# Windowed attention: values and probabilities as two rounded parts each, low keys on all 128 rows, normalisation on POOL

## The chip, the cores and the metric

One core of a Trainium2 chip. The metric is the device time of one execution in microseconds (us). The core has the engines PE (matrix products), DVE and ACT (elementwise work and copies out of PSUM, where PE leaves its results), POOL (elementwise work) and SP (here it only issues transfers). Each works through its own list of instructions in the order in which the program emits them, and semaphores between the engines hold an instruction until its inputs are there and its output's place is free.

## The reference

Two layers over 640 tokens (512 sample tokens, 128 prompt tokens) of width 1024. A layer is a SwiGLU half step, a mixer, and another half step, each followed by a LayerNorm. The mixer of layer 0 is the attention that is changed; that of layer 1 is a long convolution.

```python
def attn_latent(h, k_ctx, v_ctx, w_qkv, w_o, sink):
    q, k, v = split_qkv(h, w_qkv)          # 16 query heads, 4 key heads, 64 wide
    q, k = rope_2d(q), rope_2d(k)
...
    def block(b):                          # 128 queries
        ...
        valid = (jnp.abs(qi[:, None] - kj[None, :]) <= WINDOW) & (kj >= 0)[None] & (kj < L)[None]
        s_loc = jnp.einsum('bqkgd,bskd->bkgqs', qb, kb).astype(jnp.float32) * ATTN_SCALE
        s_loc = jnp.where(valid, s_loc, NEG_INF)
        s_ctx = jnp.einsum('bqkgd,bckd->bkgqc', qb, k_ctx).astype(jnp.float32) * ATTN_SCALE
        p = jax.nn.softmax(jnp.concatenate([s_loc, s_ctx, sink_logits(sink, B, BLOCK)], -1), axis=-1)
        o = (jnp.einsum('bkgqs,bskd->bqkgd', p[..., :S].astype(vb.dtype), vb)
             + jnp.einsum('bkgqc,bckd->bqkgd', p[..., S:S + Lc].astype(v_ctx.dtype), v_ctx))
    return o @ w_o
```

The prompt's 128 tokens attend to themselves in the same way, with no rotation and no window.

## The kernel before, in words

The program is emitted in one order for all engines, written out by hand, and each engine runs its share of it in that order. No scheduler moves anything; only pieces of LayerNorm and of the rotation (`rope`) are placed by an emission clock (`clk`, `at`, `run_due`), which counts the time of PE's products.

Products are made from float32 values in two parts that are each rounded to the type float32r: `split` copies the value into a float32r tile (the high part, on ACT) and subtracts (the low part, on DVE or POOL). A product is then three matmuls: high by high, high by low, low by high.

`attn` works in this order. `qstep` and `kstep` make the queries and keys in halves of 320 tokens; `rope` copies them from PSUM (`qs`), rotates them, and `q_hi`, `q_lo`, `k_hi`, `k_lo` write the parts. `q_lo` has two DVE operations for a half, of 320 columns for the first and of 192 for the second. Then 20 groups follow, each of four heads `g` of one block `b` of 128 queries: blocks 1 and 2 see 512 keys, blocks 0 and 3 see 384, and the prompt (block 4) sees 128. The main loop has 22 iterations of four slots. Slot i of iteration n holds, in this order:

- `tr` for chunk i of group n-2: four transposes of the probabilities `p` into the PSUM tile `pt` on PE, and a copy of it to `pts` on ACT. A group has as many chunks as its width holds 128s.
- `score` for head i of group n: two matmuls on PE (`kh` with the query, `kl` with its high half) into `s`, then on DVE one operation that adds the mask and takes the row's extreme (`tensor_tensor_reduce`, in the trace a custom operation, "p<-s,mask,sinkn"), then on ACT the exponential, which needs that extreme (`sm`).
- in the first two iterations, five steps of the values' product (`vstep`).
- `norm` of the heads of group n-1 (DVE), spread over the slots as 1, 2, 1, 0.
- `av` for an earlier chunk: one float32 matmul of `pts` with 64 columns of values, into one half of the PSUM tile `o`; the two groups of a pair (g even, g odd) fill its halves. After a pair's last chunk ACT copies `o` to `osb`, POOL makes the parts `oh` and `ol` of three heads, ACT and POOL those of the fourth.

So 58 slots hold both a chunk and a score: 28 with a score of 512 columns, 18 with 384, 12 with 128. Iterations 0 and 1 have scores without chunks, as do the slots behind a group's last chunk: after the first chunk there are 4 such scores of 512 columns, 6 of 384 and 4 of 128. After iteration N-3 the output projection's first weights are split on POOL (`w_split(nc.gpsimd, nc.gpsimd)`).

Of the kernel before, what the change touches and what calls it, by code (L numbers as in the profile page):

```python
# [15 lines left out]
P = 128  # L16
T = 640
# [25 lines left out]
class Kernel:  # L43
# [133 lines left out]
    def ada_first(self):  # L177
        """shift and scale of the first sub-layer: rows on the tensor engine, then columns"""
# [54 lines left out]
    def bg_step(self):  # L233
        """128 columns of one mod: dot products along the free dimension"""
# [22 lines left out]
    def sh(self, l, i):  # L257
        """columns for the modulated input of the sub-layer that follows LayerNorm i of layer l (i = -1: the input)"""
# [25 lines left out]
    def h_stages(self, half, k, src, G, B, first=False):  # L284
        """modulate, then split, as stages that the caller interleaves over k"""
# [26 lines left out]
    def interleave(self, chains, key=None, dt=0.0):  # L312
        """stage s of chain k in step k + s"""
# [74 lines left out]
    def ln_out(self, l, i, half, sum_t):  # L388
        """the last LayerNorm, to the output"""
# [80 lines left out]
    def rstd(self, vp, C):  # L470
        """1 / sqrt(variance + eps) of C x 4 tokens, on the diagonals of four C x C blocks"""
# [31 lines left out]
    def mm_cols(self, ps, w, c0, rhs, ks, half, first=True, last=True):  # L503
        """ps = w[:, ks, c0:c0+128]^T rhs[ks] over one half of the tokens"""
# [11 lines left out]
    def run_steps(self, steps, bg=False):  # L516
        """steps: (unit, fn(weights), last use)"""
# [101 lines left out]
    def rope(self, ps, half, hi, lo, raw_prompt):  # L619
        """rotate the sample tokens of one half, then hi(x, columns) and lo(x, columns); the prompt's stay as they are"""  # L620
# [15 lines left out]
        def add():  # L636
            nc.vector.tensor_tensor(out=qs[:, 0:n], in0=qs[:, 0:n], in1=st.pop("sh")[:, 0:n], op=ALU.add)
            hi(qs[:, 0:n], slice(a, s1))

        def low():  # L640
            lo(qs[:, 0:n], slice(a, s1))
# [5 lines left out]
    def attn(self, u0):  # L647
# [4 lines left out]
        v = fp.tile([P, 6, 256], F32, name="v")  # L652
        kp = fp.tile([P, 2, P], F32, name="kp")
        qp = fp.tile([P, KD, P], F32, name="qp")
        self.rcos = fp.tile([P, LS], F32, name="rcos")
        self.rsin = fp.tile([P, LS], F32, name="rsin")
        kc = self.t((P, 2, P), name="kc")
        nc.sync.dma_start(out=self.rcos, in_=I["k_cos"])
        nc.sync.dma_start(out=self.rsin, in_=I["k_sin"])
        nc.sync.dma_start(out=kc, in_=I["kcT"])  # L660
        nc.sync.dma_start(out=v[:, 0, :], in_=I["vc"])
# [5 lines left out]
        R = [slice(0, 64), slice(64, P)]  # L667

# [13 lines left out]
        def k_lo(x, c, t):  # L682
            for r in range(2):
                nc.vector.tensor_tensor(out=kl[R[r], t, c], in0=x[R[r]], in1=kh[t][R[r], r, c].bitcast(F32), op=ALU.subtract)

        def qstep(w, uu, half):
            self.flush(f"ln{half}")
            for j2 in range(2):
                jt = min(uu - u0, 3) * 2 + j2
                if jt not in q:  # L690
                    q[jt] = (self.b((P, LS), F32R, name="q0"), self.b((P, LS), F32R, name="q1"))
                ps = self.ps(name="q")
                self.mm_cols(ps, w, j2 * P, self.h, [(k, k) for k in range(KD)], half)
                self.rope(ps, half, lambda x, c, jt=jt: q_hi(x, c, q[jt]), lambda x, c, jt=jt: q_lo(x, c, q[jt]), qp[:, jt, :])

        def kstep(w, uu, half):
            for t in range(2):
                ps = self.ps(name="k")
                self.mm_cols(ps, w, t * P, self.h, [(k, k) for k in range(KD)], half)
                def col(c):  # L700
                    return slice(P + c.start, P + c.stop)

                self.rope(ps, half, lambda x, c, t=t: k_hi(x, col(c), t), lambda x, c, t=t: k_lo(x, col(c), t), kp[:, t, :])
# [5 lines left out]
        kl = self.rp.tile([P, 2, 768], F32R, tag="wr", name="kl")  # L709
        self.wlim = u + 6  # L710
        self.w_dma(u + 6)
        kh = [self.wp.tile([P, 2, 768], F32R, tag="w", name="kh") for _ in range(2)]
        for o in (0, 640):
            for t in range(2):
                k_hi(kc[:, t], slice(o, o + P), t)
                k_lo(kc[:, t], slice(o, o + P), t)
        self.wmax = 2
# [9 lines left out]
        def vstep(tt):  # L727
# [6 lines left out]
            nc.scalar.activation(out=v[:, 1 + tt, :], in_=ps[:, 0:256], func=AF.Copy)  # L734
            if tt == 4:
                nc.sync.dma_start(out=O["nv"], in_=v[:, 5, :])
# [5 lines left out]
        # block b of queries: first key column, width, first mask block, blocks of v  # L742
        WIN = [(0, 384, 6, [0, 1, 2]), (0, 512, 0, [0, 1, 2, 3]), (256, 512, 1, [2, 3, 4, 0]), (384, 384, 5, [3, 4, 0]), None]
# [7 lines left out]
        pts = {}  # L751

        def score(b, g, i):
            t, r = g // 2, g % 2
            jt = 4 * t + i
            rr = slice(64 * r, 64 * r + 64)
# [6 lines left out]
            if b < 4:  # L763
                c0, n, mb, _ = WIN[b]
                x = q[jt][r][:, b * P:b * P + P]
                nc.tensor.matmul(ps[:, 0:n], x, kh[t][:, r, c0:c0 + n], start=True, stop=False)
                nc.tensor.matmul(ps[:, 0:n], x[rr], kl[rr, t, c0:c0 + n], start=False, stop=True)
            else:
                n, mb = P, 0
                nc.tensor.matmul(ps[:, 0:n], qp[rr, jt, :], kp[rr, t, :])  # L770
# [9 lines left out]
        def norm(b, g, i):  # L780
# [4 lines left out]
            p = live[b, g][:, i, 0:WIN[b][1] if b < 4 else P]  # L785
            nc.vector.tensor_scalar(out=p, in0=p, scalar1=s[:, 3, i:i + 1], scalar2=None, op0=ALU.mult)
# [3 lines left out]
        def tr(b, g, c):  # L790
# [3 lines left out]
            x = self.t(name="pts")  # L794
            nc.scalar.activation(out=x, in_=pt, func=AF.Copy)
            pts[b, g, c] = x

        def av(b, g, c):
            t, r = g // 2, g % 2
            vs = WIN[b][3] if b < 4 else [5]  # L800
            if r == 0 and c == 0:
                ops[b, t] = self.ps(name="o")
            ob = ops[b, t]
            nc.tensor.matmul(ob[64 * r:64 * r + 64, :], v[:, vs[c], g * 64:(g + 1) * 64], pts.pop((b, g, c)),
                             start=(c == 0), stop=(c == len(vs) - 1))
            if c == len(vs) - 1:
                live.pop((b, g))
            if r == 1 and c == len(vs) - 1:
                ops.pop((b, t))
                osb = self.t(name="osb")  # L810
# [953 lines left out]
```

## Time and profile before

| what | value |
|---|---|
| three runs | 2789.57, 2790.73, 2800.66 us; median 2790.73 |
| the profiled execution: span | 2795.8 us |
| busy in the span: PE, DVE, ACT, POOL | 97%, 60%, 31%, 21% |
| attention's main part, 768 to 904 us: busy PE, DVE, ACT, POOL | 135.42, 83.44, 90.64, 27.31 us of 136 |

The span runs from the first instruction to the last. The page does not say which run was profiled; its span lies 5.1 us above the median of the runs, so differences are worked out against the span and then set on the median. Times in the trace count from the span's start.

### The profile page before, as it was taken

What the parts mean: (1) busy time and instruction counts of PE and PEld (TensorE: products, weight loads), DVE (VectorE), ACT (ScalarE), POOL (GpSimd) and SP (SyncE); (2) the same over time, 40 slices, a digit from 0 to 9 for tenths busy, and PEclk for the clock granted to TensorE, in tenths of its full rate; (3) what the DMA queues carried; (4) which work ended last, traced back from release to release, by engine and by line L of the source; (5) the groups of instructions that cost most, each with busy time, mean ns of one, the idle gap of its engine ahead of it and who ended that gap; (6) DMA issues with size and microseconds to landing.
All of it is one profiled execution on the core that took longest, in us unless ns stands there. A gap on an engine that the chain in (4) does not pass through costs nothing. (4 is left out here: it accounts for less than half of the span.)

```text
span 2795.8 us, 42366 instructions
## 1 busy us (share of the span) xinstructions
PE 2711.5 (97%) x17402; PEld 2529.1 (90%) x17402; DVE 1683.4 (60%) x3041; ACT 878.8 (31%) x1507; POOL 579.0 (21%) x639
## 2 busy tenths in 40 slices
PE   9989999998999999999999999999999899999997
PEld 3569999998844999999999999998998899999997
DVE  5865867748865567676766633337658856323334
ACT  3552222214565341212133121224332333122222
POOL 3541000005212420000041000005108842000002
PEclk8889999999999999999999999999999999999998
DMA  6343544421000235353522312121223321212121
GB/s 239 107 157 106 196 151 158 166 83 66 35 1 31 76 117 177 136 181 136 177 72 97 130 61 87 65 91 47 91 87 123 130 81 65 87 61 91 61 76 38
DMA packets 65017, 289.35 MB, mean 103 GB/s; under 512 B 8255, under 2 KB 13583, under 8 KB 46520
## 3 DMA queue, kind: packets, MB, share of 16 engines
q1 hardware_dynamic: 45736, 217.39, 22.2%
q0 software_dynamic: 18720, 69.21, 7.0%
q8 instruction: 137, 2.24, 0.3%
q14 instruction: 56, 0.46, 0.0%
q10 hardware_dynamic: 368, 0.04, 0.0%
HBM read 270.61 MB, written 16.01 MB: 103 GB/s over the span
## 5 line engine op out<-in xcount | busy, mean ns | idle before, releaser
L512 PE MATMUL f<-al,wh 128*128 128x320 f32 (+2 forms) x1408 | 437.2, 310 | 2.1 <-DVE al L94 1.6
L512 PE MATMUL f<-ah,wh 128*128 128x320 f32 (+2 forms) x1408 | 437.9, 311 | 0.0
L553 PE MATMUL g<-hh,wh 128*128 128x320 f32 (+1 forms) x1408 | 437.2, 310 | 0.0
L512 PE MATMUL f<-ah,wl 128*128 128x320 f32 (+2 forms) x1408 | 436.4, 310 | 0.0
L553 PE MATMUL g<-hl,wh 128*128 128x320 f32 (+1 forms) x1408 | 435.5, 309 | 0.0
L553 PE MATMUL g<-hh,wl 128*128 128x320 f32 (+1 forms) x1408 | 435.2, 309 | 0.0
L553 PE MATMUL u<-hl,wh 128*128 128x320 f32 (+1 forms) x1408 | 435.1, 309 | 0.0
L553 PE MATMUL u<-hh,wl 128*128 128x320 f32 (+1 forms) x1408 | 435.1, 309 | 0.0
L553 PE MATMUL u<-hh,wh 128*128 128x320 f32 (+1 forms) x1408 | 435.0, 309 | 0.0
L93 ACT ACTIVATE wh<-wr 128x2048 fp32r<-128x2048 f32 (+1 forms) x167 | 297.5, 1783 | 437.4 <-PE f L512 341.2
L94 DVE TENSOR_TENSOR wl<-wr,wh 128x2048 fp32r<-128x2048 f32 (+1 forms) x156 | 333.5, 2138 | 90.6 <-ACT wh L93 90.1
L563 DVE TENSOR_TENSOR ac<-sg,u 128x320 f32<-128x320 f32 (+1 forms) x176 | 85.8, 487 | 457.6 <-ACT sg L561 457.3
L561 ACT ACTIVATE sg<-g 128x320 f32<-128x320 f32 (+1 forms) x176 | 76.7, 436 | 768.1 <-PE g L553 768.1
L493 DVE SCALAR_TENSOR_TENSOR x<-f,gate,x 128x128 f32<-128x128 f32 (+3 forms) x432 | 172.1, 435 | 204.5 <-PE f L512 204.5
L512 PEld LDWEIGHTS f<-al,wh 128*128 128x128 f32 x1408 | 265.5, 189 | 3.9 <-DVE al L94 3.8
L512 PEld LDWEIGHTS f<-ah,wh 128*128 128x128 f32 x1408 | 265.7, 189 | 1.0 <-ACT ah L93 0.5
L512 PEld LDWEIGHTS f<-ah,wl 128*128 128x128 f32 x1408 | 265.6, 189 | 0.0
L553 PEld LDWEIGHTS g<-hl,wh 128*128 128x128 f32 x1408 | 264.5, 188 | 1.2 <-POOL hl L308 0.5
L553 PEld LDWEIGHTS g<-hh,wh 128*128 128x128 f32 x1408 | 264.4, 188 | 0.8 <-issue 0.3
L553 PEld LDWEIGHTS g<-hh,wl 128*128 128x128 f32 x1408 | 264.4, 188 | 0.1
L553 PEld LDWEIGHTS u<-hh,wh 128*128 128x128 f32 x1408 | 264.4, 188 | 0.0
L553 PEld LDWEIGHTS u<-hh,wl 128*128 128x128 f32 x1408 | 264.3, 188 | 0.0
(303 smaller groups left out, 4816.5 us busy)
## 6 DMA issues: line engine op xcount, KB each, us to landing
wr<-w SPq DMA_DIRECT2D x88, 1024.0 KB
ar<-ada_w POOLq DMA_DIRECT2D x128, 512.0 KB, 3.8
wr<-w2a SPq DMA_DIRECT2D x48, 768.0 KB
wr<-hyin SPq DMA_DIRECT2D x12, 1024.0 KB
wr<-ada_first SPq DMA_DIRECT2D x8, 1024.0 KB
specs<-sg SPq DMA_DIRECT2D x16, 512.0 KB
wr<-w2b SPq DMA_DIRECT2D x8, 1024.0 KB
spec<-specs SPq DMA_DIRECT2D x8, 1024.0 KB
```

What stands on the lines that cost most here:

```text
L93: nc.scalar.activation(out=hi, in_=src, func=AF.Copy)
L94: (eng or nc.vector).tensor_tensor(out=lo, in0=src, in1=hi.bitcast(F32), op=ALU.subtract)
L493: nc.vector.scalar_tensor_tensor(out=self.x[:, j, s0:s1], in0=ps[:, s0 - a:s1 - a], scalar=gate[:, tk, j:j + 1], in1=self.x[:, j, s0:s1], ...
L512: nc.tensor.matmul(ps[:, 0:z - a], s[:, kw, c0:c0 + P], m[:, a:z], start=(first and i == 0 and q == 0), stop=(last and i == n - 1 and q == 2))
L553: nc.tensor.matmul(o[:, 0:z - a], s[:, k, c0:c0 + P], m[:, a:z], start=(k == 0 and q == 0), stop=(k == 7 and q == 2))
L561: nc.scalar.activation(out=sg, in_=g[:, 0:z - a], func=AF.Silu)
L563: nc.vector.tensor_tensor(out=ac, in0=sg, in1=uu[:, 0:z - a], op=ALU.mult)
```

## The change

What it does:

- `tr` makes two parts of the probabilities: ACT's copy becomes the high part, and a new DVE operation of 128x512 subtracts it from PSUM (60 of them).
- `v` holds high and low parts side by side (128 columns for a key head). `av` has two float32r matmuls in the place of one float32 matmul; rows 64 to 127 of `o` then hold the low values' share. For each group (20) ACT copies that half (64x512) and DVE adds it to the other half, into `ob2`; the copy to `osb` (10) is gone. Each `vstep` copies to `vt` and splits (ACT, DVE) where it had one copy.
- `kl` lies on all 128 rows (the same values in both halves), so that a score is two matmuls of the same shape; the prompt's queries and keys get the same form, for which `rope` hands all 320 columns to `q_lo` and `k_lo`, and `k_lo` writes each part twice.
- `norm` runs on POOL.

The rest of the diff removes comments, and the builder is given a smaller scratch region for POOL's transfers (`dynamic_dma_scratch_size=2048`).

```diff
-    def rope(self, ps, half, hi, lo, raw_prompt):
+    def rope(self, ps, half, hi, lo):
-        nc.scalar.activation(out=qs[:, 0:n], in_=ps[:, 0:n], func=AF.Copy)
-        if s1 < z:
-            nc.scalar.activation(out=raw_prompt, in_=ps[:, n:n + LP], func=AF.Copy)
+        nc.scalar.activation(out=qs, in_=ps[:, 0:320], func=AF.Copy)
...
+        def v_split(b, src):
+            x = src.rearrange("p (g d) -> p g d", g=4)
+            nc.scalar.activation(out=v[:, b, :, 0:64], in_=x, func=AF.Copy)
+            nc.vector.tensor_tensor(out=v[:, b, :, 64:P], in0=x, in1=v[:, b, :, 0:64].bitcast(F32), op=ALU.subtract)
...
         def k_lo(x, c, t):
             for r in range(2):
-                nc.vector.tensor_tensor(out=kl[R[r], t, c], in0=x[R[r]], in1=kh[t][R[r], r, c].bitcast(F32), op=ALU.subtract)
+                for d in range(2):
+                    nc.vector.tensor_tensor(out=kl[R[d], t, r, c], in0=x[R[r]], in1=kh[t][R[r], r, c].bitcast(F32), op=ALU.subtract)
...
         def vstep(tt):
-            nc.scalar.activation(out=v[:, 1 + tt, :], in_=ps[:, 0:256], func=AF.Copy)
+            vt = self.t((P, 256), name="vt")
+            nc.scalar.activation(out=vt, in_=ps[:, 0:256], func=AF.Copy)
+            v_split(1 + tt, vt)
...
         def score(b, g, i):
+            nc.tensor.matmul(ps[:, 0:n], x, kh[t][:, r, c0:c0 + n], start=True, stop=False)
+            nc.tensor.matmul(ps[:, 0:n], x, kl[:, t, r, c0:c0 + n], start=False, stop=True)
...
         def norm(b, g, i):
-            nc.vector.tensor_scalar(out=p, in0=p, scalar1=s[:, 3, i:i + 1], scalar2=None, op0=ALU.mult)
+            nc.gpsimd.tensor_scalar(out=p, in0=p, scalar1=s[:, 3, i:i + 1], scalar2=None, op0=ALU.mult)
...
         def tr(b, g, c):
-            x = self.t(name="pts")
-            nc.scalar.activation(out=x, in_=pt, func=AF.Copy)
-            pts[b, g, c] = x
+            h, l = (self.t(dt=F32R, name="pts") for _ in range(2))
+            nc.scalar.activation(out=h, in_=pt, func=AF.Copy)
+            nc.vector.tensor_tensor(out=l, in0=pt, in1=h.bitcast(F32), op=ALU.subtract)
+            pts[b, g, c] = (h, l)
...
         def av(b, g, c):
-            nc.tensor.matmul(ob[64 * r:64 * r + 64, :], v[:, vs[c], g * 64:(g + 1) * 64], pts.pop((b, g, c)),
-                             start=(c == 0), stop=(c == len(vs) - 1))
+            for n, x in enumerate(pts.pop((b, g, c))):
+                nc.tensor.matmul(ob, v[:, vs[c], g], x, start=(c == 0 and n == 0), stop=(c == len(vs) - 1 and n == 1))
...
-                osb = self.t(name="osb")
-                nc.scalar.activation(out=osb, in_=ob, func=AF.Copy)
+            os_ = osb[b, t][R[r]]
+            low = ob2[0:64, 2 + r]
+            nc.scalar.activation(out=low, in_=ob[64:P], func=AF.Copy)
+            nc.vector.tensor_tensor(out=os_, in0=ob[0:64], in1=low, op=ALU.add)
```

How the instructions stand on the two engines behind PE is shown at one place, iteration 10 of the main loop (scores of block 2's first group `p`, chunks of a group of block 1). A row has the line, the operation, the tiles, and the engines whose semaphores the instruction waits for. ACT's list before, where L795 is the copy of a chunk, L775 the exponential, L811 the copy to `osb` and L93 the split of the fourth head:

```order
L795 ACTIVATE pts_7464<-pt_7459 128x512 [waits PE_49]
L775 ACTIVATE p_7467,sm_7466<-p_7467,sm_7466 128x512 [waits DVE_49]
L795 ACTIVATE pts_7482<-pt_7477 128x512 [waits PE_49,Pool_49]
L775 ACTIVATE p_7467,sm_7466<-p_7467,sm_7466 128x512 [waits DVE_49]
L811 ACTIVATE osb_7492<-o_7380 128x512 [waits PE_49]
L93 ACTIVATE oh_7151<-osb_7492 128x128 [waits Activation_49]
L795 ACTIVATE pts_7507<-pt_7502 128x512 [waits PE_49]
L775 ACTIVATE p_7467,sm_7466<-p_7467,sm_7466 128x512 [waits DVE_49]
```

ACT's list of the changed kernel at the same place (L808 is the chunk's high part, L788 the exponential, L830 the copy of the low half of `o`):

```order
L808 ACTIVATE pts_7590<-pt_7585 128x512 [waits PE_49,Activation_49]
L788 ACTIVATE p_7595,sm_7594<-p_7595,sm_7594 128x512 [waits DVE_49]
L808 ACTIVATE pts_7611<-pt_7606 128x512 [waits PE_49,Activation_49]
L788 ACTIVATE p_7595,sm_7594<-p_7595,sm_7594 128x512 [waits DVE_49]
L830 ACTIVATE ob2_6844<-o_7564 64x512 [waits PE_49]
L93 ACTIVATE oh_7224<-ob2_6844 128x128 [waits DVE_49]
L808 ACTIVATE pts_7639<-pt_7634 128x512 [waits PE_49,Activation_49]
L788 ACTIVATE p_7595,sm_7594<-p_7595,sm_7594 128x512 [waits DVE_49]
```

The order is the same; `oh` now waits for DVE (the sum into `ob2`), where it waited for ACT's own copy. DVE's list before, at this place (L772 is the masked score with its row extreme, L786 the normalisation):

```order
L772 ISA p_7467,sm_7466<-s_7468,mask_5872,sinkn_5873 128x512 [waits PE_49]
L772 ISA sm_7466 128x1
L783 TENSOR_TENSOR sm_7404<-sm_7404 128x4 [waits Activation_49]
L784 RECIPROCAL sm_7404<-sm_7404 128x4 [waits DVE_49]
L786 TENSOR_SCALAR p_7405<-p_7405,sm_7404 128x512 [waits DVE_49]
L772 ISA p_7467,sm_7466<-s_7484,mask_5872,sinkn_5873 128x512 [waits PE_49]
L772 ISA sm_7466 128x1
L786 TENSOR_SCALAR p_7405<-p_7405,sm_7404 128x512 x2
L772 ISA p_7467,sm_7466<-s_7509,mask_5872,sinkn_5873 128x512 [waits PE_49]
```

DVE's list of the changed kernel there (L809 is the chunk's low part, L785 the masked score, L831 the sum of the two halves of `o`):

```order
L809 TENSOR_TENSOR pts_7591<-pt_7585,pts_7590 128x512 [waits Activation_49]
L785 ISA p_7595,sm_7594<-s_7596,mask_5872,sinkn_5873 128x512 [waits PE_49,Pool_49]
L785 ISA sm_7594 128x1
L796 TENSOR_TENSOR sm_7517<-sm_7517 128x4
L797 RECIPROCAL sm_7517<-sm_7517 128x4 [waits DVE_49]
L809 TENSOR_TENSOR pts_7612<-pt_7606,pts_7611 128x512 [waits Activation_49]
L785 ISA p_7595,sm_7594<-s_7615,mask_5872,sinkn_5873 128x512 [waits PE_49]
L785 ISA sm_7594 128x1
L831 TENSOR_TENSOR ob2_6844<-o_7564,ob2_6844 64x512 [waits Activation_49]
L809 TENSOR_TENSOR pts_7640<-pt_7634,pts_7639 128x512 [waits Activation_49]
L785 ISA p_7595,sm_7594<-s_7643,mask_5872,sinkn_5873 128x512 [waits PE_49]
```

The normalisations have left the list, and ahead of every masked score stands an instruction that waits for ACT.

## Rows read from the trace of the kernel before

**Rows 1.** The page's first line: the span.

```profile
span 2795.8 us, 42366 instructions
```

**Rows 2.** Busy us (instructions) of PE, weight loads, DVE, ACT, POOL; clock; DMA.

```profile
691.00:757.00 66.00, 61.46 (x407) 59.28 (x405) 59.87 (x134) 36.01 (x88) 19.95 (x19) 0.97 0.10 35
768.00:904.00 136.00, 135.42 (x492) 59.27 (x490) 83.44 (x276) 90.64 (x241) 27.31 (x58) 1.00 0.04 16
```

**Rows 3.** Timeline of one slot, 512 columns: start, duration, [idle before <-what ended it].

```profile
821.75 0.66 PE L793 MATMUL pt<-ident,p 128*128 128x128 f32 x4
...
822.16 0.47 PE L766 MATMUL s<-kh,q 128*128 128x512 f32 x1
...
822.56 0.50 PE L767 MATMUL s<-kl,q 64*128 64x512 f32 x1
...
823.00 1.07 PE L804 MATMUL o<-pts,v 128*64 128x512 f32 x2
823.10 0.75 DVE L772 CUSTOM_DVE_ANT_0 p<-s,mask,sinkn 128x512 f32<-128x512 f32 x1 [0.68 <-PE s L767]
...
823.90 0.72 ACT L775 ACTIVATE p<-p,sm 128x512 f32<-128x512 f32 x1 [0.80 <-DVE sm L772]
...
824.00 0.66 PE L793 MATMUL pt<-ident,p 128*128 128x128 f32 x4
```

**Rows 4.** Timeline around POOL's weight split, near the end of attention.

```profile
882.49 4.53 POOL L129 TENSOR_TENSOR wl<-wr,wh 128x2048 fp32r<-128x2048 f32 x1
...
882.83 4.40 DVE L786 TENSOR_SCALAR p<-p,sm 128x384 f32<-128x384 f32 x1
...
883.91 0.66 PE L793 MATMUL pt<-ident,p 128*128 128x128 f32 x4
...
887.80 0.62 ACT L775 ACTIVATE p<-p,sm 128x384 f32<-128x384 f32 x1 [4.07 <-DVE sm L772]
...
888.42 0.57 ACT L795 ACTIVATE pts<-pt 128x512 f32<-128x512 f32 x1
```

**Rows 5.** Groups by line and shape: count | busy us, mean ns | idle us before.

```profile
L795 ACT ACTIVATE pts<-pt 128x512 f32<-128x512 f32 x60 | 35.2, 587 | 10.2 <-PE pt L793 9.7
L775 ACT ACTIVATE p<-p,sm 128x384 f32<-128x384 f32 x32 | 19.7, 615 | 16.8 <-DVE sm L772 16.5
L775 ACT ACTIVATE p<-p,sm 128x128 f32<-128x128 f32 x16 | 6.4, 400 | 4.5 <-DVE sm L772 4.3 <-DVE sm L783 0.2
L93 ACT ACTIVATE oh<-osb 128x128 fp32r<-128x128 f32 x10 | 3.1, 310 | 0.3
L772 DVE CUSTOM_DVE_ANT_0 p<-s,mask,sinkn 128x384 f32<-128x384 f32 x32 | 19.4, 615 | 19.4 <-PE s L767 19.4
L772 DVE CUSTOM_DVE_ANT_0 p<-s,mask,sinkn 128x128 f32<-128x128 f32 x16 | 5.6, 350 | 11.4 <-PE s L770 11.2
L684 DVE TENSOR_TENSOR kl<-qs,kh 64x320 fp32r<-64x320 f32 x4 | 3.0, 757 | 0.1
L684 DVE TENSOR_TENSOR kl<-qs,kh 64x192 fp32r<-64x192 f32 x4 | 2.5, 620 | 0.2 <-ACT kh L680 0.2
L684 DVE TENSOR_TENSOR kl<-kc,kh 64x128 fp32r<-64x128 f32 x8 | 2.3, 287 | 2.8 <-ACT kh L680 2.7
L444 POOL TENSOR_SCALAR o<-x,lng,lnb 128x384 f32<-128x384 f32 x4 | 2.6, 662 | 5.9 <-DVE x L435 5.7 <-DVE lv L474 0.2
```

**Rows 6.** DVE's timeline in the convolution: a subtraction of 128x512 out of PSUM.

```profile
2096.50 1.28 DVE L1337 TENSOR_TENSOR ew<-tE,ew 128x512 fp32r<-128x512 f32 x2
```

**Rows 7.** DVE's timeline where the queries are rotated: the low parts, by columns.

```profile
698.96 1.57 DVE L675 TENSOR_TENSOR q<-qs,q 64x320 fp32r<-64x320 f32 x2
...
714.10 1.03 DVE L675 TENSOR_TENSOR q<-qs,q 64x192 fp32r<-64x192 f32 x2
```

**Rows 8.** ACT's timeline: the first chunk's copy and the last score's exponential.

```profile
768.21 0.57 ACT L795 ACTIVATE pts<-pt 128x512 f32<-128x512 f32 x1
...
901.38 0.40 ACT L775 ACTIVATE p<-p,sm 128x128 f32<-128x128 f32 x1 [0.92 <-DVE sm L772]
```

More of the change, by code (lines that the diff above doesn't have):

```diff
@@ L660, in attn @@
         nc.sync.dma_start(out=kc, in_=I["kcT"])
-        nc.sync.dma_start(out=v[:, 0, :], in_=I["vc"])
+        nc.sync.dma_start(out=vc, in_=I["vc"])
         nc.sync.dma_start(out=mask, in_=I["k_mask"])
@@ L683, in k_lo @@
             for r in range(2):
[L684 removed]
+                for d in range(2):
+                    nc.vector.tensor_tensor(out=kl[R[d], t, r, c], in0=x[R[r]], in1=kh[t][R[r], r, c].bitcast(F32), op=ALU.subtract)
         def qstep(w, uu, half):
             self.flush(f"ln{half}")
+            a, z = HALF[half]
             for j2 in range(2):
@@ L690, in qstep @@
                 if jt not in q:
-                    q[jt] = (self.b((P, LS), F32R, name="q0"), self.b((P, LS), F32R, name="q1"))
+                    q[jt] = (self.b((P, T), F32R, name="q0"), self.b((P, T), F32R, name="q1"))
                 ps = self.ps(name="q")
                 self.mm_cols(ps, w, j2 * P, self.h, [(k, k) for k in range(KD)], half)
-                self.rope(ps, half, lambda x, c, jt=jt: q_hi(x, c, q[jt]), lambda x, c, jt=jt: q_lo(x, c, q[jt]), qp[:, jt, :])
+                self.rope(ps, half, lambda x, jt=jt: q_hi(x, slice(a, z), q[jt]), lambda x, jt=jt: q_lo(x, slice(a, z), q[jt]))
         def kstep(w, uu, half):
@@ L699, in kstep, with cols @@
                 self.mm_cols(ps, w, t * P, self.h, [(k, k) for k in range(KD)], half)
-                def col(c):
-                    return slice(P + c.start, P + c.stop)
-                self.rope(ps, half, lambda x, c, t=t: k_hi(x, col(c), t), lambda x, c, t=t: k_lo(x, col(c), t), kp[:, t, :])
+                def cols(f, x, t=t):
+                    if half == 0:
+                        f(x, slice(P, P + 320), t)
+                    else:
+                        f(x[:, 0:192], slice(P + 320, P + LS), t)
+                        f(x[:, 192:320], slice(2 * P + LS, 3 * P + LS), t)
+                self.rope(ps, half, lambda x, cols=cols: cols(k_hi, x), lambda x, cols=cols: cols(k_lo, x))
+                if half:
+                    nc.scalar.activation(out=kp[:, t, :], in_=ps[:, 192:320], func=AF.Copy)
         self.wlim = u + 5
@@ L708, in attn @@
             self.w_split()
-        kl = self.rp.tile([P, 2, 768], F32R, tag="wr", name="kl")
         self.wlim = u + 6
         self.w_dma(u + 6)
-        kh = [self.wp.tile([P, 2, 768], F32R, tag="w", name="kh") for _ in range(2)]
+        kh = [self.wp.tile([P, 2, 896], F32R, tag="w", name="kh") for _ in range(2)]
         for o in (0, 640):
@@ L751, in attn @@
         pts = {}
+        osb = {}
         def score(b, g, i):
@@ L762, in score @@
             h = 4 * g + i
[L763 to L770, printed above, removed]
+            c0, n, mb, _ = WIN[b]
+            x = q[jt][r][:, b * P:b * P + P]
+            nc.tensor.matmul(ps[:, 0:n], x, kh[t][:, r, c0:c0 + n], start=True, stop=False)
+            nc.tensor.matmul(ps[:, 0:n], x, kl[:, t, r, c0:c0 + n], start=False, stop=True)
             p = live[b, g][:, i]
@@ L793, in tr @@
                 nc.tensor.transpose(pt[:, i * P:(i + 1) * P], live[b, g][:, i, c * P:(c + 1) * P], self.ident)
-            x = self.t(name="pts")
-            nc.scalar.activation(out=x, in_=pt, func=AF.Copy)
-            pts[b, g, c] = x
+            h, l = (self.t(dt=F32R, name="pts") for _ in range(2))
+            nc.scalar.activation(out=h, in_=pt, func=AF.Copy)
+            nc.vector.tensor_tensor(out=l, in0=pt, in1=h.bitcast(F32), op=ALU.subtract)
+            pts[b, g, c] = (h, l)
         def av(b, g, c):
             t, r = g // 2, g % 2
[L800 to L803, printed above, removed]
-            nc.tensor.matmul(ob[64 * r:64 * r + 64, :], v[:, vs[c], g * 64:(g + 1) * 64], pts.pop((b, g, c)),
-                             start=(c == 0), stop=(c == len(vs) - 1))
[L806 to L809, printed above, removed]
-                osb = self.t(name="osb")
-                nc.scalar.activation(out=osb, in_=ob, func=AF.Copy)
+            vs = WIN[b][3]
+            if c == 0:
+                ops[b, g] = self.ps(name="o")
+            ob = ops[b, g]
+            for n, x in enumerate(pts.pop((b, g, c))):
+                nc.tensor.matmul(ob, v[:, vs[c], g], x, start=(c == 0 and n == 0), stop=(c == len(vs) - 1 and n == 1))
+            if c < len(vs) - 1:
+                return
+            live.pop((b, g))
+            if r == 0:
+                osb[b, t] = ob2[:, len(done) % 2]
+                done.append((b, t))
+            ops.pop((b, g))
+            os_ = osb[b, t][R[r]]
+            low = ob2[0:64, 2 + r]
+            nc.scalar.activation(out=low, in_=ob[64:P], func=AF.Copy)
+            nc.vector.tensor_tensor(out=os_, in0=ob[0:64], in1=low, op=ALU.add)
+            if r == 1:
+                x = osb.pop((b, t))
                 for i in range(4):
@@ L816, in av @@
                     bs = slice(b * P, b * P + P)
-                    oi = osb[:, i * P:(i + 1) * P]
+                    oi = x[:, i * P:(i + 1) * P]
                     if i == 3:
@@ L824, in attn @@
         late = []
+        done = []
+        ob2 = self.rp.tile([P, 4, 512], F32, tag="wr", name="ob2")
         N = len(groups)
```

21 lines of the change are left out of this document (11 added, 10 removed).

## The prediction

> **What bounds the kernel now.** I read the page first (a span of 2795.8 us [rows 1], PE busy 97% of it), then the windows, since the change touches one part of the kernel only. In attention's main part, 768 to 904 us, PE is busy 135.42 of 136 us at a granted clock of 1.00 (the level of 2.4 GHz), DVE 83.44, ACT 90.64 and POOL 27.31 [rows 2]: there PE is the bound, and what DVE or ACT saves is worth nothing by itself. Where queries and keys are rotated, 691 to 757 us, it is different: PE 61.46 of 66, DVE 59.87 [rows 2], both nearly full.
>
> The third view is the timeline of one slot of 512 columns [rows 3]. Matmuls overlap, so I go by starts, not by durations. On PE the transposes take 0.41 us (821.75 to 822.16), the two matmuls of the score 0.40 and 0.44, and `av` 1.00, up to the next slot's transposes at 824.00: 2.25 us. Behind PE, DVE's masked score (L772) takes 0.75, ACT's exponential starts 0.80 after the masked score's start and takes 0.72. DVE waited 0.68 for PE and ACT 0.80 for DVE: both have slack in a slot, and their work lies beside PE's.
>
> **What comes off.** DVE loses 80 normalisations, ACT ten copies to `osb`, and PE's `av` becomes two float32r matmuls for one float32 matmul. The trace has no such pair; the nearest rows are the two matmuls of a score, 0.40 and 0.44 [rows 3]. By them `av` would take 0.84 in the place of 1.00, a gain of 0.16 a slot, 9 us over 58 slots. I count PE's slot as 2.25 at most. All this pays only while PE sets the slot.
>
> **What comes in: a ring.** In DVE's new list the low part of chunk i (call it l) stands ahead of the masked score m of slot i; in ACT's, the high part h stands ahead of the exponential e, and h of the next slot behind e. l waits for h, e waits for m. If both engines keep their order, then each slot is h, l, m, e, and the next h can't start before e is through: ACT and DVE take turns, and nothing of the four overlaps. Before, only m to e was such a link; the copy waited for PE alone.
>
> Do they keep their order? [Rows 4] show it for both. A normalisation on DVE took 4.40 us while POOL split weights; the masked score behind it was late, so the exponential waited 4.07 us for DVE, until 887.80. The transposes of 883.91, whose duration is 0.66, were long ready for ACT, but their copy started at 888.42, behind the exponential. The Trainium skill ("TensorE: Matmul & The Clock Gate", "Architectural detail: the array is 16× 32×32, not 1× 128×128") states that ACT's and DVE's queues are strictly first in, first out. The trace agrees, by these 4.07 us; without that rule the kernel would go the way of the faster rival below.
>
> Price of a slot: h 0.59 [rows 5]; l from the nearest row, a subtraction of 128x512 out of PSUM, 1.28/2 = 0.64 [rows 6]; m to e 0.80; e 0.72 [rows 3]. Sum 2.75 us for 512 columns, over PE's 2.25. With 384 columns m and e are 0.615 each [rows 5], and 0.05 lies between them (0.80 - 0.75): 0.59 + 0.64 + 0.665 + 0.615 = 2.51. With 128 columns (0.350 and 0.400 [rows 5]): 0.59 + 0.64 + 0.40 + 0.40 = 2.03.
>
> - Slots with chunk and score: 28 x 2.75 + 18 x 2.51 + 12 x 2.03 = 77.0 + 45.2 + 24.4 = 146.6.
> - Scores without a chunk, now paced by ACT: 4 x 0.72 + 6 x 0.615 + 4 x 0.40 = 8.2.
> - The output of a pair, which stands in the same lists. For the first group ACT's copy of the low half (taken as a 512-column copy, 0.59) holds up the next h, while DVE's addition lies beside that h. For the second group the copy 0.59, the addition 0.64 (a 512-column operation out of PSUM) and `oh` 0.31 [rows 5], which now waits for it, follow each other. 2.13 a pair, nine pairs inside the ring: 19.2.
>
> Sum 174.0. Before, the same stretch ran from the first chunk's copy at 768.21 to the last exponential's end at 901.38 + 0.40 [rows 8], 133.6. So **+40.4**. Bounds: without the outputs, 154.8 or +21; above, each of the four links may cost a semaphore's way more, such as the 0.05 between m and e: 58 x 3 x 0.05, +9.
>
> **Ahead of it, the rotation.** DVE is near full there, so what it gains I put on the path. `q_lo`: 16 operations of the second half grow from 192 to 320 columns, each by (1.57 - 1.03)/2 = 0.27 [rows 7]: 4.3. `k_lo` writes twice: four more of 0.757 and four of 0.620 [rows 5]: 5.5. Eight for the prompt's 128 columns, between 0.287 and 0.620 [rows 5]; I take 0.38, near the row of that width: 3.0. Eight more for the cached keys at 0.287, 2.3, of which I count 0.5, since that row shows 2.8 us of waiting for ACT to fill. **+13**; 8 if some of it finds gaps, 18 with the prompt's at 0.62 and all the cached keys'.
>
> **Values.** Five `vstep`s gain a copy on ACT (0.59 at most) and a subtraction on DVE (0.64 at most), in the first two iterations between a masked score and the next one: 0 to 6.2, I take **+4**.
>
> **Normalisation on POOL.** The nearest row is a 128x384 operation of the same kind at 0.662 [rows 5], so 0.88 for 512 columns, 3.5 for a group's four. They are due one iteration later, four slots or some 11 us, so the ring hides them; with POOL's 27.31 [rows 2] there is room. Were the ring not there, four slots of PE would still cover them. One place has no cover: near the end they stand behind POOL's weight split of 4.53 [rows 4], and the transposes behind them. Before, the same split held DVE's normalisation for 4.40, so much of that is already in the time: **+1**, 0 to 4.5. Weight transfers: the DMA share is 0.04 there [rows 2], and I count nothing.
>
> **Sum:** 40.4 + 13 + 4 + 1 = +58. 2795.8 + 58 = 2853.8 for the span; the median of the runs is 2790.7 for a span of 2795.8, so the runs would give **2849 us**.
>
> **Rivals.**
>
> - *The ring holds with half its price.* The outputs fall between waits (+21), the rotation's additions half into gaps (+7 with the rest): about 2819. For it: the outputs come at different slots of a group. Against: each stands in the lists of both engines. 0.08 for 2805 to 2820.
> - *PE becomes the bound again, at a lower clock.* PE would idle 0.5 us in each slot of 2.75; before, it was without gaps at a clock of 1.00. Were PE's slots twice as long, 4.5 us, in a fifth of the 58, that adds 12 x (4.5 - 2.6) = 23: 2872. Against: the rotation's stretch, with 4.5 us of gaps in 66, kept 0.97 [rows 2]. 0.06 for 2868 to 2890.
> - *Faster: the vector engines overlap.* If a waiting instruction let the next one past, or the emission left enough distance, DVE's sum would be the bound: masked scores 32 x 0.75 + 32 x 0.615 + 16 x 0.35 = 49.3, low parts 60 x 0.64 = 38.4, additions 20 x 0.64 = 12.8, together 100.5. The main part would fall by 33 and the additions ahead and behind take 18 of it: -15, 2776. It would need PE's slot to shrink as well. The Trainium skill ("TensorEngine Tiling (Array Packing)", "Tiling Modes") says that a change of tiling mode drains TensorE; before, each score goes from 128 to 64 rows and back, and the new form doesn't. By that page PE's slot could lose more than the 0.16 above; no row here has a score of one shape. The case decides for faster once the 58 slots average under (133.6 - 18 - 8.2 - 19.2)/58 = 1.52 us. Against: [rows 4]. 0.08.
> - *No change:* slots of 1.5 to 1.8 us, gain and rotation cancelling: 2777 to 2805. 0.05.
> - *The change doesn't do what it says*, for instance `av` isn't shorter: PE's slot stays 2.25, below 2.75, and the time is that of the forecast.
>
> **How the numbers follow.** The ring as priced has 0.73 (2820 to 2868). The range, 2812 to 2872, takes in most of the half-price case and the edge of the clock's, and the bounds of the single terms: 21 + 8 + 0 + 0 = +29 or 2820 below, 49 + 18 + 6 + 4.5 = +78 or 2869 above. About 0.5% (14 us) is what a measurement of this kernel can tell from no change. Slower by more than that: 0.73 + 0.08 + 0.06 = 0.87; within it 0.05; faster 0.08.
>
> **What the changed profile would show.** Right: in the main part h to h on ACT is 2.75 us in slots of 512 columns and 2.5 in those of 384; the waits of L809 end with ACT's L808, those of the exponential L788 with DVE's L785; PE is busy clearly less than 100%, about 130 of 174 us, and idles for ACT and DVE; the first chunk's copy is some 17 us later than 768.21; the stretch to the last exponential is about 174 us. Wrong: if a slot keeps 2.25 or less while h of the next slot starts before e is through, the ring doesn't exist; if the rotation takes as long as before, DVE had room there; if POOL ends the waits of the transposes, the normalisation is what binds.

## The result and the profile after

The changed kernel takes 2864.31 us (median of 2860.47 to 2873.62), the kernel before 2791.11 in the same comparison: a ratio of 1.0263, 95% interval 1.024 to 1.0286, or 73 us more. The forecast was slower, 2849 us, in a range up to 2872.

The windows of the changed kernel, with the columns of [rows 2]: rotation, then main part.

```profile
691.00:758.00 67.00, 56.51 (x370) 55.36 (x368) 63.43 (x144) 36.92 (x82) 17.76 (x17) 0.92 0.10 34
776.00:967.00 191.00, 121.36 (x493) 88.31 (x492) 101.15 (x273) 94.86 (x246) 117.13 (x130) 0.75 0.02 6
```

Where [rows 2] had PE busy 135.42 of 136 us, it is busy 121 of 191 now, and its mean granted clock is 0.75 for 1.00. No engine is full: PE (121 us) and POOL (117, where it was 27) come nearest, DVE has 101 and ACT 95.

One slot of 512 columns in the timeline of the changed kernel, the counterpart of [rows 3]:

```profile
823.06 0.77 PE L806 MATMUL pt<-ident,p 128*128 128x128 f32 x4
...
823.48 0.58 ACT L808 ACTIVATE pts<-pt 128x512 fp32r<-128x512 f32 x1
...
824.09 0.69 DVE L809 TENSOR_TENSOR pts<-pt,pts 128x512 fp32r<-128x512 f32 x1 [1.08 <-ACT pts L808]
...
824.70 0.74 DVE L785 CUSTOM_DVE_ANT_0 p<-s,mask,sinkn 128x512 f32<-128x512 f32 x1
...
825.48 0.72 ACT L788 ACTIVATE p<-p,sm 128x512 f32<-128x512 f32 x1 [1.43 <-DVE sm L785]
...
826.20 0.58 ACT L808 ACTIVATE pts<-pt 128x512 fp32r<-128x512 f32 x1
```

High part, low part, masked score, exponential, next high part: each starts where the one before ends, and each engine waits for the other once in a slot. The slot is 2.72 us, where PE's was 2.25.

Groups by line and shape over the whole run of the changed kernel, with the columns of [rows 5]:

```profile
L808 ACT ACTIVATE pts<-pt 128x512 fp32r<-128x512 f32 x60 | 35.0, 584 | 14.1 <-PE pt L806 13.7
L788 ACT ACTIVATE p<-p,sm 128x512 f32<-128x512 f32 x32 | 23.1, 721 | 40.5 <-DVE sm L785 40.4
L809 DVE TENSOR_TENSOR pts<-pt,pts 128x512 fp32r<-128x512 f32 x60 | 41.4, 691 | 71.2 <-ACT pts L808 71.2
L785 DVE CUSTOM_DVE_ANT_0 p<-s,mask,sinkn 128x512 f32<-128x512 f32 x32 | 23.6, 741 | 0.0
L831 DVE TENSOR_TENSOR ob<-o,ob 64x512 f32<-64x512 f32 x20 | 13.7, 683 | 25.8 <-ACT ob L830 25.8
L799 POOL TENSOR_SCALAR p<-p,sm 128x512 f32<-128x512 f32 x32 | 49.6, 1563 | 34.2 <-PE pt L806 16.7 <-DVE sm L797 14.6 <-PE o L820 2.9
L799 POOL TENSOR_SCALAR p<-p,sm 128x384 f32<-128x384 f32 x32 | 39.3, 1242 | 38.6 <-DVE sm L797 29.7 <-PE s L783 5.9 <-PE pt L806 2.9
```

The ring is in the waits: DVE's low parts wait 71 us for ACT, ACT's exponentials 40 us (in this shape alone) for DVE. The masked score waits for nothing (0.0): PE's scores are always there, so PE's lower clock doesn't set these slots. The surprise is POOL: the normalisation takes 1.56 and 1.24 us where I had put 0.88 and 0.66. The group of L808 holds its price: 13.7 us of waiting for transposes. The timeline of the changed kernel shows one such wait:

```profile
812.54 3.68 POOL L799 TENSOR_SCALAR p<-p,sm 128x384 f32<-128x384 f32 x3 [6.49 <-DVE sm L797]
...
818.92 1.24 POOL L799 TENSOR_SCALAR p<-p,sm 128x384 f32<-128x384 f32 x1
...
820.22 0.48 PE L806 MATMUL pt<-ident,p 128*128 128x128 f32 x1 [3.46 <-POOL p L799]
...
820.74 0.60 ACT L808 ACTIVATE pts<-pt 128x512 fp32r<-128x512 f32 x1 [3.11 <-PE pt L806]
```

Three heads' normalisations, then a pair's output parts (between the first two rows), then the fourth head's; PE waits for it, and ACT for PE.

The marks in the changed kernel's timeline: first masked score, first high part, last exponential, output projection.

```profile
759.59 0.61 DVE L785 CUSTOM_DVE_ANT_0 p<-s,mask,sinkn 128x384 f32<-128x384 f32 x1
...
776.17 0.60 ACT L808 ACTIVATE pts<-pt 128x512 fp32r<-128x512 f32 x1 [1.28 <-PE pt L806]
...
966.35 0.39 ACT L788 ACTIVATE p<-p,sm 128x128 f32<-128x128 f32 x1
...
968.51 0.31 PE L512 MATMUL f<-oh,wh 128*128 128x320 f32 x1
```

Profiled executions differ by some 6 us in what lies ahead of attention (the rotation's first product on POOL starts at 667.12 before and 661.23 after), so I go by distances inside a trace. "Rotation" is from that product to the first masked score, "values" from there to the first high part, "stretch" from there to the output projection's first product. Before they are 89.5, 11.6 and 136.0 us, after 98.4, 16.6 and 192.3.

### The profile page after: what moved, and what is told of

It is laid out like the page before. It is cut to its first block, busy times and chain, and to the rows that moved or that the text cites. A ratio compares the mean times of both kernels' runs of the same rounds, so it can differ in the third digit from the quotient of the medians.

```text
span 2862.4 us, 42591 instructions
## 1 busy us (share of the span) xinstructions
PE 2696.0 (94%) x17402; PEld 2561.7 (89%) x17402; DVE 1715.2 (60%) x3071; ACT 891.4 (31%) x1523; POOL 674.2 (24%) x719
## 5 line engine op out<-in xcount | busy, mean ns | idle before, releaser
L93 ACT ACTIVATE wh<-wr 128x2048 fp32r<-128x2048 f32 (+1 forms) x167 | 297.6, 1783 | 441.0 <-PE f L512 330.0
L553 PEld LDWEIGHTS u<-hl,wh 128*128 128x128 f32 x1408 | 264.5, 188 | 0.0
```

Of the source, the lines that this page charges most:

```text
L93: nc.scalar.activation(out=hi, in_=src, func=AF.Copy)
L553: nc.tensor.matmul(o[:, 0:z - a], s[:, k, c0:c0 + P], m[:, a:z], start=(k == 0 and q == 0), stop=(k == 7 and q == 2))
```

## The experiments

Two theories stood beside the ring: POOL's normalisation holds the transposes (the trace puts 61 of PE's idle us down to it), or PE's lower clock sets the pace. "Changed kernel" is the kernel after the change; each run was compared with the kernel before, and the ratio is to that, with its 95% interval. A stretch is from the one trace of a run.

**The low part behind the masked score.** It opens the ring: high part and masked score can run side by side.

```diff
-            nc.vector.tensor_tensor(out=l, in0=pt, in1=h.bitcast(F32), op=ALU.subtract)
             pts[b, g, c] = (h, l)
+            return lambda: nc.vector.tensor_tensor(out=l, in0=pt, in1=h.bitcast(F32), op=ALU.subtract)
...
                 if i < nch:
-                    tr(*old, i)
+                    low_part = tr(*old, i)
                 if cur:
                     score(*cur, i)
+                if i < nch:
+                    low_part()
```

> The changed kernel with one subtraction moved: the low part of a chunk is emitted behind the slot's masked score on DVE, not ahead of it; every operation stays. Ring theory: the ring is open, high part and masked score run side by side, then low part and exponential. ACT needs 0.58 + 0.72 = 1.31 us for a slot of 512 columns, DVE 0.74 + 0.69 = 1.43, POOL, by the changed kernel's own rows, (4 x 1.56 + 2.96 / 2) / 4 = 1.93; so the slot falls from 2.74 to some 1.9 to 2.1, the main stretch from 190.6 to 140 to 150 us and the time from 2864 to 2815 (2805 to 2830). POOL theory (the normalisation on POOL holds the transposes, to which the trace puts most of PE's waiting): POOL's work is the same, so the slot stays near 2.7 and the time within 5 us of 2864. Clock theory (PE is slow because its granted clock in the stretch fell to 0.75): PE's work and order are the same, 2864 as well.

Measured: 2850.97 us, ratio to before 1.022 (1.0201 to 1.024); the stretch is 175.0. It is faster by more than the rivals allow, yet far from the 2815 of the ring theory, which was wrong as a theory of one ring. The timeline of this run shows what took over:

```profile
864.91 1.56 POOL L799 TENSOR_SCALAR p<-p,sm 128x512 f32<-128x512 f32 x1
866.53 0.48 PE L806 MATMUL pt<-ident,p 128*128 128x128 f32 x1 [3.95 <-POOL p L799]
...
868.51 1.05 PE L806 MATMUL pt<-ident,p 128*128 128x128 f32 x4
...
869.48 0.18 DVE L797 RECIPROCAL sm<-sm 128x4 f32<-128x4 f32 x1
...
869.82 6.19 POOL L799 TENSOR_SCALAR p<-p,sm 128x512 f32<-128x512 f32 x4 [3.35 <-DVE sm L797]
...
870.60 0.60 PE L806 MATMUL pt<-ident,p 128*128 128x128 f32 x4
...
870.95 0.48 PE L782 MATMUL s<-kh,q 128*128 128x512 f32 x1
...
871.26 0.40 PE L783 MATMUL s<-kl,q 128*128 128x512 f32 x1
...
871.50 0.63 PE L820 MATMUL o<-pts,v 128*128 128x512 f32 x2
...
871.96 0.60 PE L806 MATMUL pt<-ident,p 128*128 128x128 f32 x4
```

PE waits 3.95 us for the last normalisation; POOL waits 3.35 for the reciprocal, which DVE makes only in the first slot behind that wait. That is a second ring, one iteration long: reciprocal, four normalisations (and every second time a pair's output parts), transposes, first slot, reciprocal. Behind its wait PE's slots are 1.98 (with one of its four transposes) and 2.09 us (866.53, 868.51, 870.60), then 1.36 (871.96). The granted clock was 0.50 in the first (the level of 1.2 GHz), 0.64 in the second and 1.00 (2.4 GHz) in the third.

**Normalisation back on DVE**, the rest as changed:

```diff
-            nc.gpsimd.tensor_scalar(out=p, in0=p, scalar1=s[:, 3, i:i + 1], ...)
+            nc.vector.tensor_scalar(out=p, in0=p, scalar1=s[:, 3, i:i + 1], ...)
```

> The changed kernel with the normalisation back on DVE, nothing else. Ring theory: slots stay 2.74 / 2.50 / 2.01, since DVE is free while ACT makes the exponential; only the waits for POOL's normalisation go (8 us by sum over five slots, 2 us where the weight split held DVE): 2850 to 2858. POOL theory: the stretch falls towards what PE needs, some 50 us less: 2805 to 2820. Clock theory: 2864.

Measured: 2861.26 us, 1.0252 (1.0237 to 1.0268); the stretch is 187.9, 4.4 less. The slots (from the high part's start to the exponential's end) stay at 2.74, 2.50 and 2.01 us with no normalisation on POOL: the first ring alone sets them, and POOL's theory falls as the first cause. The gain of 3 us is below the 6 to 14 expected, and by the runs it isn't clear of the noise (the intervals of the two ratios overlap). Waits for POOL went, but DVE is still held beside the weight split (an exponential waits 3.27 us there), and scores without a chunk are late: behind DVE's normalisations their exponentials wait 0.2 to 0.6 us where they waited for nothing.

**Both edits together.**

> The changed kernel with the low part behind the masked score and the normalisation back on DVE. Two-rings theory (the slot's ring of ACT and DVE binds the changed kernel; where it is opened, a second ring binds, an iteration long: sum and reciprocal on DVE, four normalisations and a pair's output parts on POOL, then the transposes and with them PE): both are open here, and DVE's own work is what is left, per iteration of 512 columns 4 x (0.74 + 0.69 + 0.49) + 0.68 + 0.5 + 0.3 = 9.2 us, against 12.3 in the changed kernel and 10.6 with the low part moved alone. From the first high part to the output projection 150 to 156 us (192.3 in the changed kernel, 175.0 with the move alone), the time 2822 to 2830. Rival (PE's lower clock, not POOL, held the kernel with the move alone): no gain over it, 2846 to 2855. Rival (one ring, and POOL's work costs nothing): the same.

Measured: 2818.65 us, 1.0095 (1.008 to 1.011); the stretch is 145.2. One edit gives 13 us, the other 3, both 46: the sign of two rings, one behind the other. What is left shows in DVE's groups in this run's stretch: it waits only 7.8 us ahead of its low parts (71.2 in the changed kernel over its whole run), and is busy 128 of 145 us.

```profile
L810 DVE TENSOR_TENSOR pts<-pt,pts 128x512 fp32r<-128x512 f32 x59 | 40.5, 687 | 7.8 <-ACT pts L808 7.5
L785 DVE CUSTOM_DVE_ANT_0 p<-s,mask,sinkn 128x512 f32<-128x512 f32 x32 | 23.8, 744 | 1.2 <-PE s L783 1.1
```

**Early normalisation on POOL.** The low part moved, and `norm` of all four heads emitted ahead of an iteration's first slot.

```diff
+            if 1 <= n <= N:
+                for j in range(4):
+                    norm(*groups[n - 1], j)
             for i in range(4):
...
-                if 1 <= n <= N:
-                    for j in ((0,), (1, 2), (3,), ())[i]:
-                        norm(*groups[n - 1], j)
```

> The changed kernel with the low part behind the masked score; the normalisation stays on POOL, but a group's sum, reciprocal and four normalisations are emitted at the start of the next iteration, ahead of its first slot and of the output parts on POOL. Two-rings theory: POOL's ring loses the two places in which it waited (the first slot's masked score, and the output parts of a pair, 2.96 us); POOL's own work of 6.25 + 1.48 = 7.7 us an iteration of 512 columns is left, DVE's is 7.2: the stretch falls from 175.0 (move alone) to 135 to 150 us, the time to 2808 to 2825. Rival (PE's lower clock, or no second ring): within 5 us of the move alone, 2846 to 2855.

Measured: 2807.11 us, 1.0063 (1.0046 to 1.0079); the stretch is 138.6. Nothing but order differs from the first experiment, and 44 us are gone, so POOL's amount of work didn't hold that one, nor did PE's clock as a cause of its own: it rose with the order, from a mean of 0.78 in the stretch to 0.84.

**The price of the operation on POOL.** As the last one, with the product written with a second column.

```diff
-nc.gpsimd.tensor_scalar(out=p, in0=p, scalar1=s[:, 3, i:i + 1], scalar2=None, op0=ALU.mult)
+nc.gpsimd.tensor_scalar(out=p, in0=p, scalar1=s[:, 3, i:i + 1], scalar2=zero, op0=ALU.mult, op1=ALU.add)
```

> The kernel with early normalisation, its operation on POOL written as a product with one column and a sum with another (of zeros), the form of the row at 0.662 us for 384 columns from which the price was taken. If the form is why the one-scalar operation takes 1.24 us for the same shape, POOL's operation falls to 0.66 and 0.88, its work in an iteration of 512 columns from 7.7 to 5.0 us, DVE (7.2) is what is left, and the time falls from 2807 to 2796 to 2803. If something else sets the price (the place of input and output in memory, the other engines' work beside it), the operation stays at 1.24 and 1.56 and the time at 2807.

Measured: 2801.51 us, 1.003 (1.0019 to 1.0042); the stretch is 128.1. The form does set the price: nothing else on POOL differs from the last run, whose operations took 1.57 and 1.25 us. The groups on POOL:

```profile
L801 POOL TENSOR_SCALAR p<-p,sm,zero 128x512 f32<-128x512 f32 x32 | 24.2, 769 | 19.9 <-ACT pts L810 16.5 <-PE o L822 3.0 <-DVE sm L799 0.4
L801 POOL TENSOR_SCALAR p<-p,sm,zero 128x384 f32<-128x384 f32 x32 | 20.9, 668 | 31.8 <-PE v L750 11.6 <-ACT pts L810 8.1 <-DVE sm L799 7.2
```

**No low part of the probabilities**: the subtraction and its matmul are left out of the changed kernel.

```diff
-            h, l = (self.t(dt=F32R, name="pts") for _ in range(2))
+            h = self.t(dt=F32R, name="pts")
...
-            nc.vector.tensor_tensor(out=l, in0=pt, in1=h.bitcast(F32), op=ALU.subtract)
-            pts[b, g, c] = (h, l)
+            pts[b, g, c] = (h,)
...
```

> The changed kernel without the low part of the probabilities: the subtraction and its matmul are left out, so the output lacks that share. Ring theory: DVE no longer waits for ACT ahead of a masked score, the ring is open, and ACT (1.31 a slot) or POOL (1.93) paces: the main stretch is 135 to 150 us, the time 2808 to 2825. POOL theory: nothing on POOL changes, within 5 us of 2864. Clock theory: PE has one matmul less a slot (0.24 to 0.43 us of some 2.7), 58 slots give 14 to 25 us: 2840 to 2850.

Measured: 2835.16 us, 1.0162 (1.0147 to 1.0177); the stretch is 163.8, 10 us above what the ring theory of then allowed. The first ring is open; the waits of 3 to 4 us for normalisations at the iterations' ends stay, as in the first experiment.

**The keys alone.** The kernel before with `kl` on 128 rows and the prompt in the same form (the diff of `rope`, `k_lo` and `score` above). Of the rest of the change it has only the smaller scratch region, which no run tests alone.

> The kernel before with one part of the change: low keys on all 128 rows and the prompt in the same form (with what that adds to the rotation); values, probabilities and normalisation as before. The rotation gets about 8 us longer, as in the changed kernel. PE is the bound here. If the two matmuls of a score cost what they cost before (0.40 and 0.44), the time is 2791 + 8 = 2799 (2795 to 2804). If the change from 128 to 64 rows and back was part of that price (scores in the changed kernel stand 0.22 apart where PE runs at full clock), PE's slot loses 0.37 us, 46 slots lose 17 us, and the time is 2782 (2774 to 2790).

Measured: 2787.56 us, 0.999 (0.9981 to 1.0): inside the second range, but 5.6 us above its centre, since a slot loses 0.20 us and not 0.37. The rotation takes 97.6 us (8 more) and the stretch 124.1 (12 less). PE's timeline in this run, to be held against [rows 3]:

```profile
836.74 0.66 PE L794 MATMUL pt<-ident,p 128*128 128x128 f32 x4
837.15 0.47 PE L770 MATMUL s<-kh,q 128*128 128x512 f32 x1
837.46 0.40 PE L771 MATMUL s<-kl,q 128*128 128x512 f32 x1
837.79 1.07 PE L805 MATMUL o<-pts,v 128*64 128x512 f32 x2
838.79 0.66 PE L794 MATMUL pt<-ident,p 128*128 128x128 f32 x4
```

The score's two matmuls take 0.31 and 0.33 us where they took 0.40 and 0.44, and a slot 2.05 for 2.25. The Trainium skill ("TensorEngine Tiling (Array Packing)", "Tiling Modes") has a change of tiling mode drain TensorE. The trace agrees in sign, with 0.09 us at the change to 64 rows and 0.11 at the change back; no run tells a drain from another price of the 64-row matmul.

**Second copy of the low keys on POOL**, on top of that:

```diff
-                for d in range(2):
-                    nc.vector.tensor_tensor(out=kl[R[d], t, r, c], ...)
+                nc.vector.tensor_tensor(out=kl[R[r], t, r, c], ...)
+                nc.gpsimd.tensor_copy(out=kl[R[1 - r], t, r, c], in_=kl[R[r], t, r, c].bitcast(F32))
```

> The kernel before with the keys in the new form (as in the run with the keys alone), and the second copy of the low keys made by POOL in the place of DVE. If DVE is what the rotation waits for, its 24 operations (11.2 / 2 = 5.6 us of them beside the queries' part, 2.3 for the cached keys) come off: 2780 to 2784. If the copies on POOL hold DVE back or the keys come too late for PE: 2788 or more.

Measured: 2786.24 us, 0.9982 (0.9969 to 0.9995). The rotation falls from 97.6 to 94.6, 3 of the 5.6 us. By the medians, the 1.3 us gained over the keys alone are within the spread.

**Combinations.** The balanced kernel is the changed kernel with the order of the early normalisation, the normalisation of one head of four on ACT, the values' low parts straight from PSUM a slot later, and the second copy of the low keys on POOL. Of its diff, the part for ACT:

```diff
+            if i < 3:
                 nc.gpsimd.tensor_scalar(out=p, ...)
+            else:
+                nc.scalar.activation(out=p, in_=p, func=AF.Copy, scale=s[:, 3, i:i + 1])
```

> As the kernel with early normalisation, with the fourth head's normalisation on ACT, the values' low parts straight from PSUM and one slot later, and the second copy of the low keys made by POOL. All three engines have some 7 us of work in an iteration of 512 columns (ACT 6.8, DVE 7.1, POOL 6.2). Two-rings theory: a stretch of 120 to 135 us for 192.3, the values' steps 5 us less, the rotation 4 to 6 us less: 2780 to 2798. Rival (PE's lower clock): 2840 to 2850.

Measured: 2802.82 us, 1.0044 (1.0029 to 1.0059). The values' steps take 11.3 us for 16.6 and the rotation 95.5 for 98.4, but the stretch stays at 139.0. Then the addition of the output halves one slot later, and all high parts on POOL:

```diff
-            nc.vector.tensor_tensor(out=os_, in0=ob[0:64], in1=low, op=ALU.add)
...
+            def add():
+                nc.vector.tensor_tensor(out=os_, in0=ob[0:64], in1=low, op=ALU.add)
...
+            adds.append(add)
...
+                while adds:
+                    adds.pop(0)()
```

> The balanced kernel with the addition of the two halves of the output one slot later on DVE (its ACT copy is then done), and the fourth head's high part on POOL like the others. Output-link theory: in the balanced kernel DVE waits 1.2 to 1.3 us for ACT's copy at each of the 20 additions and ACT 0.75 us for DVE ahead of each of the 10 high parts; both go, an iteration of 512 columns falls from 8.45 to 7.4 to 7.8 us, the stretch from 139.0 to 122 to 130, the time from 2803 to 2786 to 2795. Rival (DVE's and ACT's own work with the half-clock slots is what is left): no more than 4 us, 2799 to 2803.

Measured: 2799.88 us, 1.0024 (1.0014 to 1.0034), the stretch 135.7: the rival's 3 us. The waits named are gone (DVE's ahead of the addition 1.6 us in the stretch), but ACT's exponentials then wait longer for DVE, 32.2 us in the stretch for 24.6 in the balanced kernel. And the weight split off POOL on top (`self.w_split()` for `self.w_split(nc.gpsimd, nc.gpsimd)`):

> As the one with the late addition, and the weight split near the end with its copy on ACT and its subtraction on DVE in the place of POOL. If POOL's split, beside which DVE was held 3 to 4 us in every version, costs more than 1.9 us on ACT and 2.3 on DVE: 2 to 5 us less than the one with the late addition. If not: the same within 2 us, or slower.

Measured: 2797.28 us, 1.0015 (1.0006 to 1.0024), not to be told from the last. None of these beats the kernel before. The same edit on the kernel with the keys alone and their copy on POOL:

> The kernel with the keys alone and their second copy by POOL, with the weight split near the end on ACT (copy) and DVE (subtraction) in the place of POOL, beside which a normalisation on DVE took 4.40 us before. PE waits 2.5 us for normalisations in its main part; if that is the hold, 1 to 2.5 us come off: 2784 to 2786. If the added 1.9 us on ACT and 2.3 on DVE hold PE as long: 2786 to 2788.

Measured: 2781.70 us, 0.9963 (0.995 to 0.9977), the best of all, though its interval overlaps that of the run without this edit. The stretch is 121.3 us for 124.1. Up to 102 us from its first high part the two traces agree within 0.02 us; the 2.8 us are all gained behind that, where DVE was held beside the split. PE's waits for normalisations fall from 2.5 to 0.5 us there, but its waits for ACT's copies rise from 0.7 to 2.1. The larger part is that PE is busy 19.9 us for 22.2 with the same work, at a granted clock of 1.00 where the wait had brought it down to a mean of 0.83 for 10 us. It is faster than both kernels (by 0.4% than the one before), with values, probabilities and normalisation as they were before.

## Why the prediction was right, and where its sizes were off

| term | predicted, us | measured, us |
|---|---|---|
| slot of 512, 384, 128 columns | 2.75, 2.51, 2.03 | 2.74, 2.50, 2.01 |
| first chunk to last exponential | +40.4 (ring), +1 (POOL near the end) | 190.6 - 133.6 = +57.0 |
| rotation | +13 | +8.8 |
| values | +4 | +5.0 |
| last exponential through the projection's first part | none | +0.7 |
| sum | +58 | +71.5 (runs: +73) |

**The ring held.** Order, waits and period came as worked out, with ACT's and DVE's lists in order and the masked score waiting for nothing. It is shown by two experiments from opposite sides: without POOL's work the slots stay, and with the low part moved they fall (to 1.36 us at 870.60). That the total came out 15 us from the forecast is in part luck: the rotation was charged 4 us too much, and the ring's stretch 16 too little.

**The step that was mis-sized is the normalisation on POOL**, put at +1. I took 0.662 us from a row of the same shape that has two columns as scalars; with one the operation takes 1.24 us. A group's four then take 6.2 us for 512 columns, a pair's output parts stand ahead of the fourth, and the cover of four slots fails wherever an iteration is short: L808 waits 13.7 us for transposes, 8.3 of it inside the stretch. I had looked at POOL's total and at its cover in slots of 512 columns, not at the prompt's slots of 2.0 us, nor at the ring that the normalisation closes over an iteration. One of the prediction's signs of being wrong did come: POOL ends nearly all of PE's waits ahead of transposes (55.8 of 56.1 us in the stretch). It was badly chosen, since PE had that time to spare: with the normalisation on DVE the stretch is only 4.4 us shorter.

**Smaller terms.** Beside the weight split DVE's sum of a group took 2.98 us and held an exponential 2 us longer than in its neighbours, as in [rows 4]. A pair's outputs cost 0.73 + 1.79 = 2.5 in place of 2.13, some 3 us over the seven pairs' worth that stand in slots with a chunk. Scores without a chunk wait behind an output's addition, which waits for ACT (25.8 us ahead of L831): the 8.2 us for those scores became some 12. These and POOL's 8.3 make up the 17 us.

**The rotation** was charged too high. The queries' low parts cost 26.0 us for 24.1, not 4.3 more: my two rows were of pairs in different surroundings. The new keys' copies run at 0.62 and 0.49 us where the old took 0.76 and 0.62, in all 11.2 for 5.5; the cached keys' fill ACT's wait, as assumed. With one operation for the cached values these make 8.3. (The upper bound of this term adds up to 17.1, not 18.)

**What came off PE** was charged far too low, which cost nothing here because PE didn't set the slot. At a clock of 1.00 the new `av` takes 0.46 us (871.50 to 871.96) where I had 0.84 and the old one took 1.00, the score 0.55 for 0.84, and PE's slot 1.36 for 2.25. So the faster rival's slot of 1.52 was within PE's reach.

**The rivals.** PE's clock did fall (0.75 on average), but PE didn't become the bound of this kernel. Its effect shows only where the first ring is open, in the slots behind a wait. The faster case needed an order that the program doesn't have. The early normalisation comes near it, with a stretch of 138.6 us for 136.0 before, and is still 0.6% slower: the rotation takes 10 us more and the values 4. With the cheaper operation on POOL the stretch is 128.1, 8 us under the kernel before, and rotation and values take that back.

## What to carry to other kernels

Before adding an operation between two engines that already hand work to each other, write down each engine's order for one period and look for a closed path: its period is the sum of its links, however idle the engines are, and moving one instruction behind its neighbour can open it. Then look for the next closed path, over the next longer period; opening the first was worth 13 us here alone and 46 with the second. What shortens the bounding engine's work (the keys' form, 0.20 us a slot of PE) is worth keeping apart from what loads the others: that part alone, with its copies and a weight split placed beside it, was the fastest kernel.

## What the runs showed of the hardware

- On POOL a product of a tile with one column of scalars took 1.24 us for 128x384 and 1.56 for 128x512; with a second column (a sum with zeros) 0.67 and 0.77, for more arithmetic. Why stays open.
- After a wait of 3.95 us PE's slots were 1.98 and 2.09 us, at a granted clock of 0.50 and 0.64, and then 1.36 at 1.00: here a wait for another engine cost PE more than the wait.
- At a granted clock of 1.00 the values' product took 1.00 us as one float32 matmul with 64 columns of values [rows 3], and 0.46 as two float32r matmuls with 128.
- A 128x4 sum of two SBUF operands on DVE, 0.16 us elsewhere, took 2.98 us while POOL split weights for 4.52, and ended 0.02 us behind the split.
